# Two blocks of w_up kept on chip between their two uses, and the activation table's root for two tiles of the mixer's norm

## The chip, the cores and the metric

The kernel runs on one core of one Trainium2 chip. The metric is the device time of one execution in microseconds. The profile times every instruction of one execution on the engines: PE is TensorE (matrix products), with PEld its weight loads; DVE is VectorE, ACT is ScalarE, POOL is GpSimd; SP (SyncE) issues the DMAs here, in the order in which they stand in its queue.

## The reference, cut to what matters

Two layers run over 1024 tokens of width 1024. Each has a mixer (three kinds of heads side by side, then an output product) and an MLP; the residual is added after a norm:

```
x = x + g_m * _rmsnorm(y, norm_g[l, 1])          # y: the mixer's output
h = _rmsnorm(x, norm_g[l, 2]) * (1.0 + sc_f) + sh_f
y = jnp.square(jax.nn.relu(h @ w_up[l])) @ w_down[l]
x = x + g_f * _rmsnorm(y, norm_g[l, 3])
```

`w_up[l]` has 1024 rows and 4096 columns. All of it is in f32; the kernel writes each f32 operand as a high and a low part and makes three matrix products of one (`mm3`, L189 to L193).

## The kernel before, in words

**Scheduling.** The Python program says in which order instructions are written and which addresses they use. A scheduler then orders them on each engine by a simulated time; each engine, and SP's DMA queue, runs its own list strictly in order and waits on semaphores.

**Space.** Working tiles come from one arena of 17,856 words per partition (`F_WORDS`). `F.get(a, b)` takes a free run of a·b words, the one released longest ago in program order, and `F.put` releases it. Whoever writes a run again has to wait for the last reader of what lay there before. A load is therefore issued no earlier than the release of its place, and everything behind it in SP's queue waits with it.

**The end of the mixer (`mixer`, L1357).** Tokens are handled in tiles of 128. `out_proj` (L1301) makes the output product of a tile, squares it for the norm (L1321), loads the residual (L1324), forms the inverse root of the mean square (L1327), scales and adds (L1328, L1329) and stores (L1330). Tiles 6 and 7 are the last; their sum and a scratch tile stay on chip (`kept`, four runs of 1024 words). The inverse root is `rsqrt`, L165 to L171: for one column nine small DVE instructions, each needing the one before. The other norms use `rstd` (L182 to L186): a square root on ACT and four small DVE instructions. `renorm` (L1336) loads a tile again (L1346; tiles 6 and 7 are taken from `kept`), norms it (L638 or L636, then L639) and transposes it on PE.

**The up product with fewer multiplications (`mlp_up`, L233).** Tokens are in two halves, the rows of `w_up` in two halves, and its columns in 16 pairs of 128-column groups. For a pair, the four quarter blocks are called a11, a12, a21, a22. The product of a pair is made as two *plain* products (a11 and a12 with the first half of the tokens) and five products of *sums* of blocks with sums of the token blocks. The token sums, called T here, are built by `transp_late` (L200) from tiles 4 to 7: POOL adds (L207, L209), a transpose on PE (L212), DVE differences and splits (L644, L217, L231). The block sums of a pair are made on POOL (L284, L285, L287, L290). Each of the seven operands is split into a high part by ACT (L230) and a low part by DVE (L231) and waits in a ring of four places for its product, twelve matmuls on PE.

**The order in `mlp_up`.** Since T needs the last token tiles, the plain products of the first six pairs (`LEAD`) are made first, interleaved with `renorm` of tiles 4 to 7 (`late`). Then follow the sums of pairs 0 to 5, and from pair 6 on plain and sums together. `todo` lists these 22 steps; `stage` (L265) takes the next one, gets a place and issues its load (L270), one step ahead of `forms` (L273), which yields the split operands. For the first six plain steps only the 128 needed columns are loaded (1024 words, 512 KB); for a sums step, or a whole pair, both groups (2048 words, 1 MB). So pairs 0 to 5 are loaded twice: half, then whole. A plain product leaves `p1` (512 words) in the arena until its sums; results go through two activations (L246, L247) to DRAM (L248).

Of the kernel before, what the change touches and what calls it, by code (L numbers as in the profile page):

```python
# [17 lines left out]
P = 128  # L18
T = 1024
NT = T // P  # L20
D = 1024
KD = D // P
# [3 lines left out]
RMS_EPS = 1e-6  # L26
# [4 lines left out]
WOW = 16  # L31
GROUPS = [2] + [4] * 6 + [2, 4]
LEAD = 6
C_Q, C_K, C_V, C_CQ, C_CKV, C_KR, C_Z, C_XBC, C_DT = 0, 256, 512, 768, 1024, 1152, 1184, 1696, 2464

SLOT = 2048
# [70 lines left out]
class Net:  # L107
# [125 lines left out]
    def mlp_up(self, l, hT, bg, late):  # L233

        nc, F = self.nc, self.F
        w_up = self.i["w_up"][l].rearrange("(k p) f -> p k f", p=P)
        hh, hl = hT
        half = slice(0, 512), slice(512, 1024)  # L240
        B = lambda k, n: tuple(h[:, k * 4:k * 4 + 4, half[n]] for h in hT)
        dma = nc.sync.dma_start

        def store(f, hf, t):

            nc.scalar.activation(t, t, AF.Relu)  # L246
            nc.scalar.activation(t, t, AF.Square)  # L247
            dma(self.d_r[l][f, :, half[hf]], t)  # L248
            F.put(t)


        ring = [tuple(h[:, k, half[1]].rearrange("p (k f) -> p k f", f=P) for h in hT) for k in range(4)]
        turn = [0]

        def cut(src):
            r = ring[turn[0] % 4]
            turn[0] += 1
            self.split(src, *r)
            return r

        N = FF // (2 * P)
        todo = [(i, True, False) for i in range(LEAD)] + [(i, i >= LEAD, True) for i in range(N)]
        staged = []

        def stage():  # L265

            if todo:
                i, plain, sums = todo.pop(0)
                st = F.get(KD, 2 * P if sums else P)
                dma(st, w_up[:, :, i * 2 * P:i * 2 * P + st.shape[2]])  # L270
                staged.append((st, plain, sums))

        def forms():  # L273

            stage()
            st, plain, sums = staged.pop(0)
            a11, a12 = st[:, 0:4, 0:P], st[:, 4:8, 0:P]
            if plain:
                yield cut(a11)
                yield cut(a12)  # L280
            if sums:
                a21, a22 = st[:, 0:4, P:2 * P], st[:, 4:8, P:2 * P]
                s1, s2 = F.get(4, P), F.get(4, P)
                nc.gpsimd.tensor_add(s1, a21, a22)  # L284
                nc.gpsimd.tensor_sub(s2, s1, a11)  # L285
                yield cut(s2)
                nc.gpsimd.tensor_sub(a21, a11, a21)  # L287
                yield cut(a21)
                yield cut(s1)
                nc.gpsimd.tensor_sub(s2, a12, s2)  # L290
                yield cut(s2)
                F.put(s1, s2)
                yield cut(a22)
            F.put(st)

        stage()
        parts = self.chain(*(forms() for _ in range(LEAD + N)))
        queue = [next(parts) for _ in range(3)]

        def product(b):  # L300

            q = next(parts, None)
            if q is not None:
                queue.append(q)
            w, ps = queue.pop(0), self.bank()
            for k in range(4):
                self.mm3(ps, w[0][:, k], w[1][:, k], b[0][:, k], b[1][:, k], k == 0, k == 3)
            return ps

        add = nc.vector.tensor_add  # L310
        T = [tuple(t[:, a] for a in range(2)) for t in self.sums()]
        p1 = {}

        def plain(i):
            ps, p = product(B(0, 0)), F.get(512)
            nc.scalar.copy(p, ps)
            ps, c = product(B(1, 0)), F.get(512)
            add(c, p, ps)
            store(2 * i, 0, c)
            p1[i] = p  # L320

        def sums(i):
            f, p = 2 * i, p1.pop(i)
            ps, u2 = product(T[1]), p
            add(u2, p, ps)
            ps, u3 = product(T[2]), F.get(512)
            add(u3, u2, ps)
            ps = product(T[0])
            add(u2, u2, ps)
            c = F.get(512)  # L330
            add(c, u3, ps)  # L331
            store(f + 1, 1, c)
            ps = product(B(1, 1))
            add(u2, u2, ps)
            store(f, 1, u2)
            ps = product(T[3])
            add(u3, u3, ps)
            store(f + 1, 0, u3)

        for i in range(LEAD):  # L340
            next(late, None)
            next(late, None)
            plain(i)
        self.drain(late)
        for i in range(N):
            if i >= LEAD:
                plain(i)
            sums(i)
            if i > 1:
                next(bg, None)  # L350
                next(bg, None)
# [949 lines left out]
    def out_proj(self, l, t, st, cc, src, dst, g, cT, keep=None):  # L1301

        nc, F = self.nc, self.F
        wo = st["wo"]
        for gg in range(2):
            a = cc[:, 512 + gg * 256:768 + gg * 256]
            nc.gpsimd.tensor_scalar(a, a, st["yrs"][:, 2 * t + gg:2 * t + gg + 1], None, op0=ALU.mult)
        self.transp8(cc, cT[0], cT[1], 0, True)
        if t % 2:
            F.put(st["cc"].pop(t // 2))  # L1310
        yield 1.0
        u = F.get(D)
        ss = self.sm(2, "fss")
        for dh in range(2):
            dd = slice(dh * 512, dh * 512 + 512)
            y = self.bank()
            for k in range(KD):
                self.mm3(y, cT[0][:, k], cT[1][:, k], wo[k][:, 0, dd], wo[k][:, 1, dd], k == 0, k == KD - 1)
                if k % 2:
                    yield 1.3  # L1320
            nc.scalar.activation(u[:, dd], y, AF.Square, accum_out=ss[:, dh:dh + 1])  # L1321
            nc.scalar.copy(u[:, dd], y)
        x = F.get(D)
        nc.sync.dma_start(x, src[t * P:t * P + P])  # L1324
        s = self.sm(1, "fs1")
        nc.vector.tensor_add(s, ss[:, 0:1], ss[:, 1:2])
        rs = self.rsqrt(s, 1, 1.0 / D, RMS_EPS)  # L1327
        nc.vector.scalar_tensor_tensor(u, in0=u, scalar=rs, in1=g, op0=ALU.mult, op1=ALU.mult)  # L1328
        nc.vector.tensor_add(x, x, u)  # L1329
        nc.sync.dma_start(dst[t * P:t * P + P], x)  # L1330
        if keep is None:
            F.put(x, u)
        else:
            keep[t] = x, u
# [262 lines left out]
```

## Time and profile before

| | us |
|---|---|
| time, median of 3 runs | 2828.76 (2823.73 to 2833.22) |
| the profiled execution's own time | 2827.39 |
| its span, first to last instruction | 2825.7 |
| PE busy | 2642.5 |
| DVE busy | 1755.9 |
| ACT busy | 1111.0 |
| POOL busy | 587.5 |

The up product starts at about 743 us in the first layer and at about 2133 us in the second. A row of the timeline reads: start, duration, engine (a q behind it: the queue that issues), line, operation, tiles written and read, shape, number of instructions merged, and in brackets how long the engine had been idle before it and what released it. A row of the windows reads: the stretch, its length, and for each engine its busy time and its instructions, then the granted TensorE clock (1.00 is full), the DMA engines' busy share and the rate. A row of the waits reads: who waited for whom, the microseconds in total, how often, and the longest.

### The profile page before, as it was taken

To read this page: it belongs to the slowest core of one execution; us is meant where nothing else is said; L and a number is where in the kernel's file an instruction comes from. 1 tells how busy PE (TensorE), PEld (TensorE's weight loads), DVE (VectorE), ACT (ScalarE), POOL (GpSimd) and SP (SyncE) were. 2 spreads that over 40 slices of the span, in tenths; PEclk is the share of its full clock that TensorE was granted. 3 is DMA by queue.
4 is the path that set the end of the run, shared out by engine and by line. 5 is a ranking of instruction groups with operands and counts; after the bars stand their busy time and mean duration, and the time that the engine had idled before them with its cause. 6 is when DMAs were issued, how large, how long until landed. Compare 5 with 4: busy or idle time off the path is not lost.

```text
span 2825.7 us, 34756 instructions
## 1 busy us (share of the span) xinstructions
PE 2642.5 (94%) x12530; PEld 2066.1 (73%) x12530; DVE 1755.9 (62%) x3223; ACT 1111.0 (39%) x2145; POOL 587.5 (21%) x517
## 2 busy tenths in 40 slices
PE   5799999899879999999999999988997999999998
PEld 4677776676757777777778777765766888888886
DVE  7767666544867777756585576664459654643435
ACT  5243443544534446121143433354445455621212
POOL 1441233310333220000021113342003522000002
PEclk9899988899989999999999998888998999999999
DMA  6441212322345546534331121132133432541313
GB/s 225 116 137 51 94 50 61 110 73 84 101 150 165 158 148 216 179 122 151 107 119 48 56 91 63 54 101 86 52 105 104 153 116 101 177 149 65 120 47 102
DMA packets 268527, 311.54 MB, mean 110 GB/s; under 512 B 28674, under 2 KB 212164, under 8 KB 268356
## 3 DMA queue, kind: packets, MB, share of 16 engines
q1 hardware_dynamic: 268356, 309.32, 34.0%
q8 instruction: 99, 1.62, 0.2%
q14 instruction: 72, 0.59, 0.1%
HBM read 242.85 MB, written 66.43 MB: 109 GB/s over the span
## 4 chain that ended last, share of the span: by engine, by line
PE 65%; DVE 11%; DMA 7%; issue 2%; ACT 2%; POOL 1%; SPq 0%; DVEq 0%; ACTq 0%; POOLq 0%
PE bank_b L191 9%; PE bank_b L193 9%; PE bank_b L192 9%; PE bank_s L191 8%; PE bank_s L192 8%; PE bank_s L193 8%; PE bank_s L962 3%; DVE split L231 2%; PE bank_a L909 2%; PE bank_t L922 2%; DVE arena_f L570 2%; DMA arena_f<-in_w_ada 1%; DMA d_r<-arena_f 1%; PE bank_s L656 1%; PE bank_a L938 1%
## 5 line engine op out<-in xcount | busy, mean ns | idle before, releaser
L191 PE MATMUL bank_b<-split 128*128 128x512 f32 (+2 forms) x1824 | 728.5, 400 | 51.0 <-ACT split L230 33.1
L192 PE MATMUL bank_b<-split 128*128 128x512 f32 (+2 forms) x1824 | 709.6, 389 | 3.5 <-DVE split L231 3.1
L193 PE MATMUL bank_b<-split 128*128 128x512 f32 (+2 forms) x1824 | 706.5, 389 | 2.9 <-DVE split L231 2.9
L230 ACT CAST split<-arena_f 128x512 fp32r<-128x512 f32 (+1 forms) x424 | 305.8, 747 | 678.3 <-PE bank_s L192 425.8
L191 PE MATMUL bank_s<-split 128*128 128x512 f32 (+2 forms) x1152 | 456.1, 398 | 18.3 <-DVE arena_f L390 6.7
L192 PE MATMUL bank_s<-split 128*128 128x512 f32 (+2 forms) x1152 | 451.2, 392 | 4.4 <-DVE split L231 1.8
L191 PEld LDWEIGHTS bank_b<-split 128*128 128x128 f32 x1824 | 354.1, 194 | 129.5 <-ACT split L230 34.8
L193 PE MATMUL bank_s<-split 128*128 128x512 f32 (+2 forms) x1152 | 448.2, 389 | 0.0
L231 DVE TENSOR_TENSOR split<-arena_f,split 128x512 fp32r<-128x512 f32 (+1 forms) x424 | 381.7, 919 | 92.8 <-ACT split L230 92.0
L193 PEld LDWEIGHTS bank_b<-split 128*128 128x128 f32 x1824 | 352.7, 193 | 71.6 <-DVE split L231 5.0
L192 PEld LDWEIGHTS bank_b<-split 128*128 128x128 f32 x1824 | 354.7, 194 | 68.5 <-issue 4.9
L408 DVE TENSOR_TENSOR arena_f<-arena_f,bank_s 128x1024 f32<-128x1024 f32 x126 | 153.5, 1218 | 230.9 <-PE bank_s L193 230.9
L191 PEld LDWEIGHTS bank_s<-split 128*128 128x128 f32 (+1 forms) x1152 | 218.4, 190 | 73.8 <-DVE arena_f L390 7.4
L192 PEld LDWEIGHTS bank_s<-split 128*128 128x128 f32 (+1 forms) x1152 | 219.5, 191 | 50.4 <-DVE split L231 3.5
L193 PEld LDWEIGHTS bank_s<-split 128*128 128x128 f32 (+1 forms) x1152 | 219.1, 190 | 43.4 <-issue 0.2
L897 ACT ACTIVATE arena_f<-bank_s,nm 128x128 f32<-128x128 f32 (+3 forms) x192 | 141.8, 740 | 191.8 <-DVE nm L896 160.8
L896 DVE TENSOR_REDUCE nm<-bank_s 128x1 f32<-128x128 f32 (+3 forms) x192 | 142.2, 752 | 118.8 <-PE bank_s L1111 64.5
L570 DVE SCALAR_TENSOR_TENSOR arena_f<-arena_f,cond 128x128 f32<-128x128 f32 x448 | 161.7, 387 | 71.4 <-DMA arena_f<-in_b_ada 32.9
L246 ACT ACTIVATE arena_f<-arena_f 128x512 f32<-128x512 f32 x128 | 80.8, 632 | 141.6 <-DVE arena_f L331 69.6
L962 PE MATMUL bank_s<-split 32*128 32x512 f32 (+3 forms) x576 | 124.0, 390 | 12.3 <-ACT arena_f L897 9.1
L925 ACT COPY arena_f<-bank_t 128x512 f32<-128x512 f32 (+1 forms) x160 | 86.8, 542 | 114.1 <-PE bank_t L922 100.9
L696 POOL TENSOR_TENSOR arena_f<-arena_f 128x1024 f32<-128x1024 f32 x14 | 33.6, 2399 | 454.0 <-ACT rstd_y L182 340.0
(281 smaller groups left out, 3207.0 us busy)
## 6 DMA issues: line engine op xcount, KB each, us to landing
arena_f<-in_w_ada SPq DMA_DIRECT2D x80, 512.0 KB
d_r<-arena_f SPq DMA_DIRECT2D x128, 256.0 KB
arena_f<-in_w_up SPq DMA_DIRECT2D x32, 1024.0 KB
arena_f<-in_w_down SPq DMA_DIRECT2D x64, 512.0 KB
arena_f<-d_r SPq DMA_DIRECT2D x64, 512.0 KB
arena_f<-d_x SPq DMA_DIRECT2D x36, 512.0 KB
d_x<-arena_f SPq DMA_DIRECT2D x23, 512.0 KB
arena_f<-in_w_in SPq DMA_DIRECT2D x20, 512.0 KB
```

Source lines behind the costliest of these rows:

```text
L191: mm(out, wh, xh, start=start, stop=False)
L192: mm(out, wh, xl, start=False, stop=False)
L193: mm(out, wl, xh, start=False, stop=stop)
L230: self.nc.scalar.copy(hi, src)
L231: (eng or self.nc.vector).tensor_sub(lo, src, f32(hi))
L246: nc.scalar.activation(t, t, AF.Relu)
L408: nc.vector.tensor_add(y[t], y[t], ps)
L570: nc.vector.scalar_tensor_tensor(acc, in0=w[:, k], scalar=self.cond[:, k:k + 1], in1=acc, op0=ALU.mult, op1=ALU.add)
L896: nc.vector.tensor_reduce(nm, S[:, 0:n], axis=AX.X, op=ALU.max, negate=True)
L897: nc.scalar.activation(p[:, 0:n], S[:, 0:n], AF.Exp, bias=nm, accum_out=ls)
L925: nc.scalar.copy(held, ps[:, 0:w])
L962: nc.tensor.matmul(S[mp][:, c0:c1], Q[rw, a, tok], K[rw, b, c0:c1], start=a == b, stop=a == 1 and c1 < n)
```

## The change

The first two plain steps (`KEEP = 2`) load the whole pair, 2048 words and 1 MB instead of 1024 words and 512 KB. They don't release it; it is held in `whole` until the sums of that pair, which take it from there and issue no load. And `out_proj` of tiles 6 and 7 (those with `keep`) calls `rstd` instead of `rsqrt`.

```diff
+KEEP = 2
...
         todo = [(i, True, False) for i in range(LEAD)] + [(i, i >= LEAD, True) for i in range(N)]
-        staged = []
+        staged, whole = [], {}
...
                 i, plain, sums = todo.pop(0)
-                st = F.get(KD, 2 * P if sums else P)
-                dma(st, w_up[:, :, i * 2 * P:i * 2 * P + st.shape[2]])
-                staged.append((st, plain, sums))
+                keep = i < KEEP and not sums
+                if i in whole:
+                    st = whole.pop(i)
+                else:
+                    st = F.get(KD, 2 * P if sums or keep else P)
+                    dma(st, w_up[:, :, i * 2 * P:i * 2 * P + st.shape[2]])
+                if keep:
+                    whole[i] = st
+                staged.append((st, plain, sums, keep))
...
-            st, plain, sums = staged.pop(0)
+            st, plain, sums, keep = staged.pop(0)
...
-            F.put(st)
+            if not keep:
+                F.put(st)
...
-        rs = self.rsqrt(s, 1, 1.0 / D, RMS_EPS)
+        rs = self.rsqrt(s, 1, 1.0 / D, RMS_EPS) if keep is None else self.rstd(s)
```

## The prediction

> **What bounds the kernel now.** I read the page first, then who waited for whom on PE around the start of each up product, then the timeline of each engine there, and last the windows for the clock.
>
> ```profile
> span 2825.7 us, 34756 instructions
> PE 2642.5 (94%) x12530; PEld 2066.1 (73%) x12530; DVE 1755.9 (62%) x3223; ACT 1111.0 (39%) x2145; POOL 587.5 (21%) x517
> ...
> PE bank_b L191 <- ACT split L230: 20.9, 2, 19.0
> ```
>
> PE is busy 94% of the span, so a change that adds or takes little PE work can only act where PE stands idle or runs slowly. The third row is PE's longest wait between 700 and 850 us: 19.0 us at one matmul, for a split weight. Its place is the step from the plain products to the sums:
>
> ```profile
> 784.78 1.04 PE L212 MATMUL bank_s<-ident,arena_f 128*128 128x128 f32 x8
> 804.84 0.79 PE L191 MATMUL bank_b<-split 128*128 128x512 f32 x1 [19.02 <-ACT split L230]
> ...
> 2176.92 1.04 PE L212 MATMUL bank_s<-ident,arena_f 128*128 128x128 f32 x8
> 2185.60 0.79 PE L191 MATMUL bank_b<-split 128*128 128x512 f32 x1 [7.65 <-ACT split L230]
> 2189.45 0.79 PE L192 MATMUL bank_b<-split 128*128 128x512 f32 x1 [3.06 <-DVE split L231]
> ```
>
> In both layers PE ends the plain products with the transposes of token tile 7 (L212), at 785.8 and 2178.0, and then waits for the first sums. Behind the split stands POOL, which makes the block sums, and behind POOL the load:
>
> ```profile
> 774.16 1.37 POOL L209 TENSOR_TENSOR arena_f<-arena_f 128x512 f32<-128x512 f32 x1
> 791.70 1.44 POOL L284 TENSOR_TENSOR arena_f<-arena_f 128x512 f32<-128x512 f32 x1 [16.17 <-DMA arena_f<-in_w_up]
> ...
> 801.53 1.26 POOL L284 TENSOR_TENSOR arena_f<-arena_f 128x512 f32<-128x512 f32 x1
> ...
> 2180.63 1.52 POOL L284 TENSOR_TENSOR arena_f<-arena_f 128x512 f32<-128x512 f32 x1 [15.92 <-DMA arena_f<-in_w_up]
> ...
> 729.39 0.34 SPq L1346 DMA_DIRECT2D arena_f<-d_x  x1
> ...
> 743.50 0.38 SPq L270 DMA_DIRECT2D arena_f<-in_w_up  x1
> ...
> 770.14 0.38 SPq L270 DMA_DIRECT2D arena_f<-in_w_up  x1
> ...
> 785.85 0.38 SPq L270 DMA_DIRECT2D arena_f<-in_w_up  x1
> ...
> 792.27 19.81 SPq L270 DMA_DIRECT2D arena_f<-in_w_up  x4
> ...
> 2162.15 0.38 SPq L270 DMA_DIRECT2D arena_f<-in_w_up  x1
> ...
> 2173.24 1.12 SPq L270 DMA_DIRECT2D arena_f<-in_w_up  x2
> ...
> 2191.14 8.93 SPq L270 DMA_DIRECT2D arena_f<-in_w_up  x2
> ```
>
> The row at 770.14 is the half load of pair 5, the last plain one; those from 785.85 on are whole. The first whole load goes out at 785.85, when PE is already done, and POOL gets it at 791.70: 5.85 us for 1 MB. PE's first sums product starts 3.3 us behind the L284 at 801.53, the third, so by the times the pair that PE needs came third. In the second layer the pair comes first, issued at 2173.24. Either way the load, not the work, is late.
>
> The idle time also costs clock:
>
> ```profile
> 804.80:809.40 4.60, 4.21 (x9) 2.91 (x10) 4.00 (x3) 1.24 (x2) 2.29 (x2) 0.50 0.00 0
> ...
> 2185.60:2195.20 9.60, 6.54 (x15) 4.78 (x16) 9.06 (x8) 1.76 (x3) 6.51 (x4) 0.50 0.29 93
> 860.00:980.00 120.00, 115.27 (x502) 89.87 (x501) 93.88 (x194) 54.22 (x97) 37.08 (x39) 1.00 0.51 162
> ```
>
> At full clock a matmul takes 115.27/502 = 0.23 us. In the first stretch, at clock 0.50, PE got 9 done by 809.4, worth 2.1 us; so the sums stand as if they had started at full clock at 807.3. In the second layer: 15 by 2195.2, worth 3.45 us, as if started at 2191.75.
>
> **Part 1: the loads that go.** With the change, pairs 0 and 1 lie in the arena when the sums begin; per layer two 1 MB loads leave SP's queue, and two 512 KB loads become 1 MB. The wait for the load goes entirely. What is late next is T, the token sums, of which tile 7 is the last part; it comes from DVE, and DVE is full:
>
> ```profile
> 743.40:780.80 37.40, 33.88 (x147) 27.10 (x146) 36.64 (x60) 22.38 (x41) 13.52 (x6) 0.91 0.23 78
> ...
> 2135.30:2173.20 37.90, 32.53 (x142) 26.02 (x141) 37.79 (x68) 22.97 (x41) 10.16 (x6) 0.93 0.20 69
> ...
> 785.04 0.69 DVE L318 TENSOR_TENSOR arena_f<-arena_f,bank_b 128x512 f32<-128x512 f32 x1 [4.26 <-PE bank_b L193]
> 785.86 0.69 DVE L644 TENSOR_TENSOR arena_f<-bank_s,arena_f 128x512 f32<-128x512 f32 x1
> ...
> 790.74 2.96 DVE L231 TENSOR_TENSOR split<-arena_f,split 128x512 fp32r<-128x512 f32 x3
> ```
>
> DVE works 36.64 of 37.40 us up to the norm of tile 7, and 37.79 of 37.90 in the second layer. So however the steps are reordered, T is ready no earlier than this work plus what is left: the add at 785.04 (0.7 us), tile 7's instructions from 785.86 to the first of the three last splits at about 791.7 (5.9 us, T for the first product), and two weight splits of about 0.7 us (1.4). That is 8.0 us, less 1.1 us from part 2: 6.9 us. First layer: 780.8 + 6.9 = 787.7, against 807.3: **-19.6 us**. Second layer: 2173.2 + 6.9 = 2180.1, against 2191.75: **-11.65 us**. PE, done at 785.8 and 2178.0, then waits about 2 us.
>
> **Part 2: the root.** For tiles 6 and 7 nine small DVE instructions become four and a root on ACT:
>
> ```profile
> 742.83 0.14 DVE L165 TENSOR_SCALAR rs_m<-fs 128x1 f32<-128x1 f32 x1
> ...
> 746.71 0.27 DVE L170 TENSOR_SCALAR rs_t<-rs_y,rs_m 128x1 f32<-128x1 f32 x1
> ...
> 765.84 1.27 DVE L1328 SCALAR_TENSOR_TENSOR arena_f<-arena_f,rs_y 128x1024 f32<-128x1024 f32 x1
> ...
> 776.01 0.14 DVE L183 TENSOR_SCALAR rstd_m<-nss 128x1 f32<-128x1 f32 x1
> ...
> 779.50 1.28 DVE L639 SCALAR_TENSOR_TENSOR arena_f<-arena_f,rstd_y 128x1024 f32<-128x1024 f32 x1
> ```
>
> The five instructions saved are 0.14 to 0.27 us each: 0.7 to 1.35 us a tile, I take 1.1. Much more is their queueing: between larger work, the nine take from 742.83 to 765.84, 23 us; the same tile's `rstd` takes 3.5 us (776.01 to 779.50). So tile 7's chain can end up to 19 us earlier. This frees no DVE time, which is why part 1 goes by DVE's total; but it lets the transposes of tile 7 stand ahead of the last plain products on PE. Without it T would come as now, 791.7. The root adds one small instruction to ACT, which works 22.38 of 37.40 us there: nothing. I count no table load for it, since `renorm` takes roots in the same stretch.
>
> **Part 3: what the held pairs cost.** In front: the up loads are ahead of the load of a token tile in SP's queue (729.39), for which ACT waited:
>
> ```profile
> 734.27 1.06 ACT L638 ACTIVATE split<-arena_f 128x1024 fp32r<-128x1024 f32 x1 [3.05 <-DMA arena_f<-d_x]
> ...
> 741.45 1.97 PE L212 MATMUL bank_s<-ident,arena_f 128*128 128x128 f32 x8 [3.15 <-DVE arena_f L639]
> ```
>
> PE's wait of 3.15 us stands behind that norm. A further 512 KB ahead of it takes 0 (hidden) to 5.85/2 = 2.9 us; I take 1.5 a layer: **+3 us**. The larger cover is that the first product starts at 743 and the first load goes out at 711.
>
> In the middle: POOL's sums for pairs 0 and 1, now at 791 to 806 beside idle engines, will run when POOL is free, from 775.5, beside full DVE. That this costs DVE time:
>
> ```profile
> 2180.95 5.10 DVE L217 TENSOR_TENSOR arena_f<-arena_f 128x512 f32<-128x512 f32 x3
> 2185.98 8.82 DVE L231 TENSOR_TENSOR split<-arena_f,split 128x512 fp32r<-128x512 f32 x7
> ```
>
> These ten, beside POOL's block sums, took 13.9 us; ten at the 0.69 us of the L644 row would take 6.9. The bounds are 0 and the difference, 7.0 us a layer. I take 2.5, nearer to 0, since part of POOL's sums can fall behind T: **+5 us**. The Trainium skill speaks against the change here: "SBUF — State Buffer", section "Who interferes with whom", says that a DVE instruction with two SBUF inputs contends with a GpSimd instruction that reads SBUF, by an exclusive lock held for the whole instruction. By that rule the sums' full duration would be DVE's loss; the trace agrees in kind (1.39 us each against 0.69).
>
> Space: the two held pairs take 4096 of 17,856 words, and 3072 more than before lie there during the plain products. By counting gets and puts about 1,950 words stay free at the tightest point, so later half loads may get places that are released later. If they do not, nothing; if they do, the rivals below.
>
> **The sum.** -19.6 - 11.65 + 3 + 5 = -23.2 us. The profiled execution took 2827.39 us, 1.4 us less than the median of 2828.76. 2827.39 - 23.2 = 2804.2; against the median 2805.6. I predict **2806**; its own range, with the bounds of the front and POOL terms (not all at their ends at once), is 2796 to 2816.
>
> **The rivals.**
> *DVE does not bind.* If the order lets T be ready when PE ends, and pair 5's half load stops being late, the sums start with the plain end less the idle that its late load (770.14) makes today:
>
> ```profile
> 774.89 0.50 PE L191 MATMUL bank_b<-split 128*128 128x512 f32 x1 [1.84 <-ACT split L230]
> 778.32 0.79 PE L193 MATMUL bank_b<-split 128*128 128x512 f32 x1 [1.69 <-DVE split L231]
> ...
> 2167.50 0.50 PE L191 MATMUL bank_b<-split 128*128 128x512 f32 x1 [4.56 <-ACT split L230]
> ```
>
> That is 785.8 - 3.5 = 782.3 and 2178.0 - 4.6 = 2173.4: -25.0 - 18.4 + 3 = -40, 2788. Against it stand the full DVE rows.
> *POOL takes DVE's time in full*: 7.0 instead of 2.5 us a layer, -14.2 us, 2815. For it: POOL has nothing else to do from 775.5.
> *Pair 5's half load falls one place back* in the line of loads, to 785.85 and 2173.24, since its space is held. From issue to the end of the plain products it was 785.8 - 770.14 = 15.7 us and 15.8 us. They would then end at 801.5 and 2189.0: -5.8 - 2.7 + 3 = -5.5, 2823: no change that can be told.
> *Slower: it falls two or three places back*, to the later loads of the same line (792.27 and the one behind it; 2191.14). The plain products end at about 808.4 and 2206.9: +1.1 + 15.2 + 3 = +19, 2848. This decides from an issue later than 791.6 in the first layer (807.3 less 15.7) and 2175.9 in the second. For it: loads wait for places today already. Against: by program order the places of tile 6 and of two earlier half loads are released before it.
>
> **How the numbers follow.** Chances: forecast 0.52, DVE not binding 0.11, POOL in full 0.13, one place back 0.12, two or more 0.12. The measurement can tell about 0.3%, 8.5 us. Faster: 0.52 + 0.11 + 0.09 of the POOL case = 0.72. Same: the other 0.04 and one place back, 0.16. Slower: 0.12. The range runs from 2790, inside the best case, to 2825, behind one place back; it leaves out the slower case and half of the best one.
>
> **What would show it.** Right: no wait of PE above 5 us at the first sums product; four loads of w_up fewer; POOL's first L284 ahead of PE's last plain product; clock 1.00 where it was 0.50; tile 7's L1328 some 10 to 19 us nearer to its square. Wrong: an idle PE in front of the plain products of pairs 2 to 5 with a load of w_up behind it (space), or PE waiting for L217 or L231 by more than 8 us (DVE), or an L212 of tile 4 later than 743 (front).

## The result: slower by half a per cent, and the profile after

| | before | after |
|---|---|---|
| median of 12 runs each, us | 2826.45 (2818.20 to 2836.52) | 2841.55 (2829.22 to 2856.83) |
| ratio, 95% interval | | 1.0054 (1.0029 to 1.0080) |
| the profiled execution: its time, its span | 2827.39, 2825.7 | 2842.88, 2841.2 |

The change costs about 15 us; forecast was a gain of 23. The head of the page of after:

```profile
span 2841.2 us, 34709 instructions
...
PE 2653.4 (93%) x12530; PEld 2072.1 (73%) x12530; DVE 1759.5 (62%) x3203; ACT 1113.1 (39%) x2149; POOL 581.2 (20%) x517
```

PE has the same 12530 instructions and DVE and ACT the intended 20 fewer and 4 more; PE's busy time grew by 11 us. Of this some 7 is clock: PE was busy at half clock for 226 us, in before for 211, and half of the 15 more is time lost. Lines of after are one higher than those of before up to about L264 and seven or eight higher behind. PE's longest waits between 700 and 850 us:

```profile
PE bank_b L192 <- ACT split L231: 15.6, 3, 14.0
PE bank_b L194 <- DVE split L232: 2.3, 1, 2.3
```

Still one long wait for a split weight, 14.0 us in place of 19.0. But it stands elsewhere. PE's timeline of after, both layers (in brackets the idle time and its releaser):

```profile
775.30 0.79 PE L192 MATMUL bank_b<-split 128*128 128x512 f32 x1 [13.97 <-ACT split L231]
...
778.78 0.79 PE L194 MATMUL bank_b<-split 128*128 128x512 f32 x1 [2.26 <-DVE split L232]
...
2170.52 4.92 PE L213 MATMUL bank_s<-ident,arena_f 128*128 128x128 f32 x24 [6.07 <-DVE rstd_y L187]
...
2189.32 0.79 PE L192 MATMUL bank_b<-split 128*128 128x512 f32 x1 [13.87 <-ACT split L231]
...
2206.67 0.50 PE L193 MATMUL bank_b<-split 128*128 128x512 f32 x1 [3.31 <-DVE split L232]
```

The wait at the first sums is gone: in the first layer the last plain add runs at 794.4 and the first add of the sums at 795.6. The new 14 us stand ahead of the *plain* product of pair 4, in both layers. What PE waited for there, on ACT (first layer):

```profile
761.29 2.70 ACT L231 CAST split<-arena_f 128x512 fp32r<-128x512 f32 x5 [7.12 <-DMA arena_f<-in_w_up]
...
774.64 1.65 ACT L231 CAST split<-arena_f 128x512 fp32r<-128x512 f32 x3
```

The split at 774.64 waits for the semaphore of the load that SP issued at 770.11, 512 KB for pair 4 (SP's list has the six loads in the order 3, 2, 0 whole, 1 whole, 5, 4). SP's timeline and, behind it, its longest wait for such a load:

```profile
757.30 13.20 SPq L275 DMA_DIRECT2D arena_f<-in_w_up  x2
```
```profile
SPq L275 <- DVE split L232: 19.5, 3, 12.4
```

SP held that load back for 12.4 us until DVE's low part L232 of a token tile had left its place. By the arena's addresses pair 4's half load got 1024 words of which half had just been one of tile 5's working tiles (the others a finished plain result, already stored); in before it got the token rows of tile 4, which come free a tile earlier, and it was pair 5's half load that got working tiles of tile 5. While PE idled, its clock fell; windows of after:

```profile
764.80:781.90 17.10, 4.34 (x9) 2.98 (x10) 17.07 (x19) 6.83 (x12) 9.00 (x6) 0.50 0.15 47
...
2178.00:2195.00 17.00, 5.68 (x13) 4.33 (x14) 15.90 (x21) 8.57 (x16) 6.92 (x5) 0.50 0.29 83
```

Clock 0.50 for 17 us in each layer, where before had 0.50 around the first sums. DVE worked 17.07 of 17.10 us: the places that SP waited for came free at DVE's pace.

**Stretches.** To compare kernels I cut each profiled execution at five marks: first plain copy of the up product, start of the down product, first norm of the second layer's output product, first plain copy of the second layer, start of its down product. PE's idle time is the length of a stretch less PE's busy time in the windows.

| us | up, layer 0 | down 0 and mixer 1 | output product 1 | up, layer 1 |
|---|---|---|---|---|
| before | 352.4 | 863.3 | 175.2 | 320.7 |
| after | 348.3 | 876.5 | 185.4 | 328.5 |

Only the first column gained, by 4.1 us. The other three lost 13.2, 10.2 and 7.8, and the first two of these lie ahead of the second layer's up product.

### The profile page after: what moved, and what is told of

Same layout as the page of the kernel before. It is cut to its first block, busy times and chain, and to the rows that moved or that the text cites. A ratio compares the mean times of both kernels' runs of the same rounds, so it can differ in the third digit from the quotient of the medians.

```text
span 2841.2 us, 34709 instructions
## 1 busy us (share of the span) xinstructions
PE 2653.4 (93%) x12530; PEld 2072.1 (73%) x12530; DVE 1759.5 (62%) x3203; ACT 1113.1 (39%) x2149; POOL 581.2 (20%) x517
## 5 line engine op out<-in xcount | busy, mean ns | idle before, releaser
L232 DVE TENSOR_TENSOR split<-arena_f,split 128x512 fp32r<-128x512 f32 (+1 forms) x424 | 385.1, 929 | 94.1 <-ACT split L231 88.3
L905 ACT ACTIVATE arena_f<-bank_s,nm 128x384 f32<-128x384 f32 (+4 forms) x192 | 142.1, 742 | 187.1 <-DVE nm L904 152.7
L578 DVE SCALAR_TENSOR_TENSOR arena_f<-arena_f,cond 128x128 f32<-128x128 f32 x448 | 155.4, 378 | 76.9 <-DMA arena_f<-in_w_ada 46.9
L970 PE MATMUL bank_s<-split 32*128 32x512 f32 (+3 forms) x576 | 122.9, 386 | 10.5 <-ACT arena_f L905 7.2
```

What stands on the lines that cost most here:

```text
L232: (eng or self.nc.vector).tensor_sub(lo, src, f32(hi))
L578: nc.vector.scalar_tensor_tensor(acc, in0=w[:, k], scalar=self.cond[:, k:k + 1], in1=acc, op0=ALU.mult, op1=ALU.add)
L905: nc.scalar.activation(p[:, 0:n], S[:, 0:n], AF.Exp, bias=nm, accum_out=ls)
L970: nc.tensor.matmul(S[mp][:, c0:c1], Q[rw, a, tok], K[rw, b, c0:c1], start=a == b, stop=a == 1 and c1 < n)
```

## The experiments

Two theories at the start. *Space*: the held pairs push later loads onto late places. *Root*: the new root delays something at the end of the mixer. All ratios below are to runs of before that alternate with them on the same chip (medians 2821.98 to 2823.23, 23 to 29 runs each), for 6 to 12 runs of each kernel; that of after is the one above. The kernels ran in groups, each on another chip, so between groups the ratios compare better than the times.

**One part alone.** `keep_only` holds the pairs and keeps the old root:

```diff
-        rs = self.rsqrt(s, 1, 1.0 / D, RMS_EPS) if keep is None else self.rstd(s)
+        rs = self.rsqrt(s, 1, 1.0 / D, RMS_EPS)
```

> The change with its loads alone: pairs 0 and 1 held, the old root (nine DVE instructions) in out_proj. Space theory (the held places push the load of token tile 5 and the half load of pair 4 behind the token sums of tile 4 and 5): slower than before by 8 to 25 us, with PE waits over 8 us in front of a plain product in at least one layer. Root theory (the new root reorders the engines and delays the last tiles; the loads alone help): faster by 10 to 25 us, no PE wait over 5 us between the first plain product and the first sums.

`root_only` has the root and holds nothing; the diff of the pairs is undone.

> The change with its root alone: no pair held, all loads as before. Space theory: -6 to +2 us, the wait at the first sums still there (15 to 20 us in the first layer, 5 to 10 in the second). Root theory: slower by 10 to 25 us.

Measured: pairs alone 2812.76, ratio 0.9955 (0.9930 to 0.9979); root alone 2826.72, 1.0006 (0.9986 to 1.0026). So neither part alone is slower. With the pairs held, adding the root costs 28.8 us. That is no sum of two separate costs, and both theories missed. Space is not enough: the pairs alone show the same wait of 14.46 and 13.82 us ahead of pair 4 and still gain. Nor is the root: alone it should have cost 10 to 25 us, and no change can be told.

**Space without data.** `space_only` (old root) holds the places of pairs 0 and 1 but loads only halves into them, releases them at the sums and loads the pairs whole into places free by then:

```diff
-                    st = whole.pop(i)
+                    F.put(whole.pop(i))
+                    st = F.get(KD, 2 * P)
+                    dma(st, w_up[:, :, i * 2 * P:i * 2 * P + 2 * P])
...
-                    dma(st, w_up[:, :, i * 2 * P:i * 2 * P + st.shape[2]])
+                    c = 2 * P if sums else P
+                    dma(st[:, :, 0:c], w_up[:, :, i * 2 * P:i * 2 * P + c])
```

> The places of the change without its saved loads: pairs 0 and 1 get 2048 words each at their plain step and hold them until their sums, but only the half is loaded there, and the whole is loaded again for the sums into a new place, as before; old root. Space theory: slower than before by 15 to 40 us, the same late loads as in the change (token tile 5 and the half load of pair 4 issued 10 us or more later than before against the first plain product) and a wait at the first sums besides. Root theory, or a theory by which the size of the first loads is at fault: within 5 us of before.

2802.47, ratio 0.9920 (0.9893 to 0.9946): 20 us faster, a clear miss of both theories on the time. In the first layer PE does wait 16.64 us ahead of pair 4's plain product, for a split of a half load issued only at 767.35, as the space theory expected; in the second no such wait is left. The wait for the first whole load goes here too, since the load finds a place that has been free for long and goes out before the plain products end. So keeping the *data* isn't what removes that wait. A long stretch far from the change is short as well: down 0 and mixer 1 took 841.7 us.

**One pair.** `last_one` (new root) holds only pair 5 and makes its sums first:

```diff
-KEEP = 2
+KEEP = 1
...
-        todo = [(i, True, False) for i in range(LEAD)] + [(i, i >= LEAD, True) for i in range(N)]
+        order = [*range(LEAD - KEEP, LEAD), *range(LEAD - KEEP), *range(LEAD, N)]
+        todo = [(i, True, False) for i in range(LEAD)] + [(i, i >= LEAD, True) for i in order]
...
```

> Only the last plain pair (5) is loaded whole and held, and its sums come first, before those of pairs 0 to 4; new root. Nothing is held while tiles 4 to 7 are worked on up to the place of pair 5's own load. Space theory: faster than before by 8 to 25 us, since the wait at the first sums goes and no token load is late; pair 5's load takes about 2 us longer. Root theory: slower by 5 to 20 us, as the change.

2807.86, 0.9961 (0.9939 to 0.9982): 15 us faster, as the space theory forecast here. Less space held, no wait above 7.2 us in either up product; again mixer 1 is short, 847.4 us.

**A first try at the far stretch.** The working tiles of the second layer's mixer get other addresses when the first layer's up product ends in another state of the arena. The addresses of after and `keep_only` are the same there (876.5 and 877.1 us), as are those of before and `root_only` (863.3 and 863.3), which looked like a cost of 13 us for places. `same_places` is after with a list of 793 addresses of before, `keep_places` the same in `keep_only`:

```diff
...
-        at = self._find(m, top)
+        k, self.count = self.count - 677, self.count + 1
+        at = PLACES[k] if 0 <= k < len(PLACES) else None
+        if at is None or any(self.used[at:at + m]):
+            at = self._find(m, top)
```

> After, with one thing undone: from the sixth block load of layer 0's sums to the end of layer 1's mixer the arena hands out the addresses of before (a fixed list), so the mixer of layer 1 has before's places again; held pairs and root stay. Theory of places: the stretch from layer 0's down product to layer 1's first output norm takes 863 us plus or minus 3 as in before (863.4) and with the root alone (863.3), not 876.4 as in after and 877.1 with the pairs alone; the time is about 13 us under after, near 2828 (1.000 to 1.002 of before). Rival, chance of the clock: the 13 us are where the half clock fell in two profiled executions; the stretch lies anywhere from 860 to 880 and the median stays with after, 2838 to 2842 (1.004 to 1.006).

> The same list of addresses in the kernel that holds the pairs but keeps the old root. Theory of places: the stretch falls from 877.1 to 863 plus or minus 3 and the time from 2812.8 to about 2800 (0.990 to 0.993 of before). Rival, chance of the clock: the time stays at 2810 to 2815 (0.995 to 0.997).

`forgotten` is before with one line more behind the first layer's down product:

```diff
+            F.stamp = [0] * F.n
```

> Before, without any part of the change; only the arena forgets after layer 0's down product when each run of words was released, so that the mixer of layer 1 gets other places. Same work, same loads. Theory of places: that stretch's 841.7, 847.4, 863 and 877 us in four placements say that placement alone moves it by some 10 us either way; the ratio to before leaves 1.000 by over 0.003 and the whole difference lies in layer 1's mixer. Rival: places do not matter where nothing is held; 1.000 plus or minus 0.003.

Measured: `same_places` 2838.54, 1.0042 (1.0023 to 1.0060), the stretch 872.0; `keep_places` 2827.18, 1.0026 (1.0003 to 1.0049), the stretch 862.2; `forgotten` 2819.14, 0.9994 (0.9977 to 1.0012), the stretch 867.8. The theory falls in this form: the times did not follow. Two reasons are visible. The list began inside the first layer's up product and made that longer, 360.8 and 351.3 us against 348.3 and 341.1 in the kernels it was put into. And the 13 us were mostly clock: by the granted clock, after ran 113 us of the stretch at half clock, before 85, `same_places` with before's addresses 106; half of such time is lost. PE idled *less* in after, as these two windows show:

```profile
1099.50:1962.80 863.30, 824.61 (x3965) 642.03 (x3965) 543.37 (x1071) 295.91 (x603) 150.38 (x138) 0.95 0.33 104
```
```profile
1082.70:1959.20 876.50, 844.99 (x3977) 656.50 (x3977) 555.60 (x1084) 296.62 (x605) 148.84 (x141) 0.94 0.32 103
```

Before, then after: 863.30 less 824.61 is 38.7 us idle, 876.50 less 844.99 is 31.5.

**More space.** `returned` releases the scratch of tiles 6 and 7 and the gain row before the up product:

```diff
-            keep[t] = x, u
+            F.put(u)
+            keep[t] = x
...
-            x, u = src[t]
+            x, u = src[t], F.get(D)
...
+        F.put(g)
...
-        F.put(g, *nxt)
+        F.put(*nxt)
```

> After, but the scratch tiles of tiles 6 and 7 and the gain row (3072 words) are released before the up product instead of at its late part, so the loads of pairs 4 and 5 get places that come free one tile earlier. Theory of space: the wait of 14 us ahead of pair 4's plain product (13.97 us in layer 0, 13.87 in layer 1) falls to 7 us or less in both layers, and from the first plain copy to the down product layer 0 takes 341 or less (348.3 in after), layer 1 322 or less (328.5). Rival, VectorE is the bound there: its token work ends no sooner, the wait stays at 12 to 14 us and moves by less than 2. The total is not forecast closely, since the mixer of layer 1 gets other places too: 2815 to 2840.

2844.36, 1.0072 (1.0044 to 1.0100). The wait on a late load is gone in both layers; others took its place, the longest 7.46 us for a DVE add in the first layer, 6.65 and 6.35 in the second. The up products took 350.7 and 321.4: the second as forecast, the first not; the time is above the forecast 2815 to 2840.

**What the root delays.** Now I laid the two kernels with the same addresses, after and `keep_only`, side by side, at the end of the second layer's mixer. ACT of after:

```profile
2104.83 1.04 ACT L646 ACTIVATE split<-arena_f 128x1024 fp32r<-128x1024 f32 x1
2105.78 0.19 ACT L646 ACTIVATION_READ_ACCUMULATOR split<-arena_f 128x1 f32 x1
2112.74 0.60 ACT L1329 ACTIVATE arena_f<-bank_b 128x512 f32<-128x512 f32 x1 [6.78 <-PE bank_b L194]
...
2119.86 0.30 ACT L183 ACTIVATE rstd_y<-fs,eps 128x1 f32<-128x1 f32 x1
...
2120.95 0.48 ACT L183 ACTIVATE rstd_y<-nss,eps 128x1 f32<-128x1 f32 x2
```

ACT of `keep_only`, the same place:

```profile
2093.80 0.19 ACT L646 ACTIVATION_READ_ACCUMULATOR split<-arena_f 128x1 f32 x1
2093.89 0.47 ACT L183 ACTIVATE rstd_y<-nss,eps 128x1 f32<-128x1 f32 x2
2099.50 0.60 ACT L1329 ACTIVATE arena_f<-bank_b 128x512 f32<-128x512 f32 x1 [5.14 <-PE bank_b L194]
```

L646 are the squares of token tiles 2 and 3, the two L183 on `nss` their roots. In `keep_only` they follow at once. In after the root of tile 6 (`fs`) stands ahead of them in ACT's list, and it needs tile 6's output product. ACT idles 6.78 us with two roots at hand, and they run 15 us after their squares. DVE's norms of these two tiles and SP's queue follow; DVE of after, then SP of after:

```profile
2105.62 1.28 DVE L647 SCALAR_TENSOR_TENSOR arena_f<-arena_f,rstd_y 128x1024 f32<-128x1024 f32 x1
2115.89 1.29 DVE L652 TENSOR_TENSOR arena_f<-bank_s,arena_f 128x512 f32<-128x512 f32 x2 [8.98 <-PE bank_s L664]
...
2125.27 2.48 DVE L647 SCALAR_TENSOR_TENSOR arena_f<-arena_f,rstd_y 128x1024 f32<-128x1024 f32 x2
```
```profile
2124.72 0.34 SPq L1338 DMA_DIRECT2D d_x<-arena_f  x1
2131.94 0.37 SPq L275 DMA_DIRECT2D arena_f<-in_w_up  x1
2134.42 0.34 SPq L1354 DMA_DIRECT2D arena_f<-d_x  x1
2146.38 0.34 SPq L1338 DMA_DIRECT2D d_x<-arena_f  x1
...
2160.82 0.32 SPq L1354 DMA_DIRECT2D arena_f<-d_x  x1
```

The norms at 2125.27 let PE transpose tiles 2 and 3, which frees the place of the whole load at 2131.94; behind that stands the load of token tile 4 (2134.42), behind its work that of tile 5 (2160.82), and PE's wait of 6.07 us for tile 5's root at 2170.52. `keep_only` is 12.0 us earlier at the end of the last square, but 24.0 and 24.1 us earlier at the two token loads (2110.43 and 2136.71): 12 us are lost on the way.

Why is tile 6's root ahead? `rstd` takes its three one-column tiles by name from sets of four. In the order in which the program is written, tile 6's root comes between those of tiles 1 and 2; if the scheduler gives out the tiles of one set in that order, the roots of tiles 2 and 3 can't be put ahead of tile 6's. The old root drew from sets of its own and could be passed. This was inferred from the order of the instructions; the next run tests it. `own_tiles` is after with one thing changed:

```diff
-    def rstd(self, ssq, y=None):
+    def rstd(self, ssq, y=None, own=False):
...
+        if own:
+            m, t = (self.small.tile([P, 16], F32, tag=f"rs_{c}", name=f"rs_{c}", bufs=3)[:, 0:1] for c in "mt")
+            y = self.sm(1, "rs_y")
...
-        rs = self.rsqrt(s, 1, 1.0 / D, RMS_EPS) if keep is None else self.rstd(s)
+        rs = self.rsqrt(s, 1, 1.0 / D, RMS_EPS) if keep is None else self.rstd(s, own=True)
```

> After, pairs held and root kept, but the root of tiles 6 and 7 takes its three one-column tiles from the sets that the old root used, not from the set that the roots of tiles 0 to 5 share. Theory of the shared set: in after ScalarE's root of tile 6 (2119.86 us, it waits for the output product) stands in its list ahead of the roots of tiles 2 and 3, whose squares were done at 2105.97; their norms run at 2125.27, and the load of token tile 5 goes out at 2160.82. With sets of their own those two roots pass: the norms run within 3 us of the squares, the load of token tile 5 goes out about 12 us earlier against the products, and the time falls to that of the pairs alone or a little under, 2804 to 2816 (0.992 to 0.997 of before). Rival, the pairs and the root both ask for space or for ScalarE: the time stays at 2830 to 2842 (1.002 to 1.006).

2805.83 (2799.82 to 2816.24), ratio 0.9941 (0.9921 to 0.9961), inside the forecast: 35.7 us under after, or 32 by the two ratios. ACT of `own_tiles` (L650 and L187 are the square and the root):

```profile
2084.10 1.04 ACT L650 ACTIVATE split<-arena_f 128x1024 fp32r<-128x1024 f32 x1
2085.05 0.19 ACT L650 ACTIVATION_READ_ACCUMULATOR split<-arena_f 128x1 f32 x1
2085.14 0.47 ACT L187 ACTIVATE rstd_y<-nss,eps 128x1 f32<-128x1 f32 x2
2090.77 0.60 ACT L1333 ACTIVATE arena_f<-bank_b 128x512 f32<-128x512 f32 x1 [5.16 <-PE bank_b L198]
...
2097.86 0.30 ACT L187 ACTIVATE rs_y<-fs,eps 128x1 f32<-128x1 f32 x1
```

The two roots run directly behind their squares and tile 6's comes last. SP of `own_tiles` sends token tile 4 at 2101.73, ahead of the store of tile 6, and tile 5 at 2127.64:

```profile
2101.73 0.34 SPq L1358 DMA_DIRECT2D arena_f<-d_x  x1
2106.04 14.26 SPq L1342 DMA_DIRECT2D d_x<-arena_f  x2
...
2127.64 0.32 SPq L1358 DMA_DIRECT2D arena_f<-d_x  x1
```

From the last square (2105.78 and 2085.05) to tile 5's load it is 42.6 us, against 55.0 in after: the 12 us are back. In the first layer it is 36.3 against 46.9. The Trainium skill states the condition, in "PSUM — Partial Sum Buffer", section "Engine vs sequencer instructions": the queues of ScalarE, VectorE and GpSimd are strictly first in, first out. The rows agree: ACT idled 6.78 us with ready work behind a waiting instruction.

The same edit in three other kernels: the root without pairs (`root_own`), `last_one` (`last_own`), and `space_only`, which thereby gets the new root (`space_own`).

> The root alone, no pair held, with tiles of its own as well. Theory of the shared set: the 8 us that the root alone costs at full clock (2696 against 2688) go; 2812 to 2822 (0.996 to 1.000 of before) where the root with shared tiles gave 2826.7. Rival: the short root is worth nothing either way; 2823 to 2830.

> The kernel that holds only pair 5 and sums it first (2807.9 with the shared set), with tiles of its own for the root. Theory of the shared set: some 5 to 10 us less, 2796 to 2804 (0.990 to 0.994 of before). Rival: no change, 2804 to 2812.

> The kernel that only holds the places of pairs 0 and 1 and loads them twice (2802.5 with the old root), with the root in tiles of its own. Theory of the shared set: the root in its own tiles costs nothing; 2795 to 2805 (0.990 to 0.994 of before). Rival, the root itself brings the loss of the change: 2815 or more.

Measured: `root_own` 2806.65, 0.9946 (0.9922 to 0.9970), 20 us under `root_only` and more than forecast; `last_own` 2805.24, 0.9939 (0.9919 to 0.9958), only 2.6 us under `last_one`, a miss; `space_own` 2787.61, 0.9883 (0.9850 to 0.9916), 15 us under `space_only` and better than forecast, though the two ratios' intervals overlap. `own_tiles` and `root_own` show the cost of the shared set, and `root_own` that the root in its own tiles is a gain over before's; `last_own` shows no cost. `root_own` holds nothing and is as fast as `own_tiles`: once the root has its own tiles, the held pairs bring no difference that can be told. So the two parts don't add up: with nothing held the root's gain, 15 us, and the shared set's cost, 20 us, nearly cancel, while with the pairs held the cost is far larger than the gain.

The traces show where the cost comes from in some of these. In the second layer of `root_only` the two roots are held up too, from the last square at 2094.53 to 2109.32, and token tile 5's load goes out at 2123.41; in `root_own` that load goes out at 2099.5. In `last_one` they are held up as long, from 2082.88 to 2097.03, but that load had gone out at 2083.41, ahead of them.

**What is left of space.** In `own_tiles` PE still waits ahead of pair 4:

```profile
769.72 0.80 PE L196 MATMUL bank_b<-split 128*128 128x512 f32 x1 [12.34 <-ACT split L235]
...
2155.22 0.80 PE L196 MATMUL bank_b<-split 128*128 128x512 f32 x1 [12.77 <-ACT split L235]
```

`returned_own` joins `returned` and `own_tiles`. `own_far` is `own_tiles` with a list of 691 addresses of `space_own`, from the last third of the first layer's up product to the end of the second layer's mixer, so behind the place where the first lists did harm; `before_far` is before with the same list.

> Pairs held, root in its own tiles, and the 3072 words of tiles 6 and 7's scratch and the gain row released before the up product, so that the loads of pairs 4 and 5 get places that come free one tile earlier. Theory of space: the wait on a split behind a block load ahead of pair 4's plain product, 12.3 us in layer 0 and 12.8 in layer 1 with the places of after, is gone or under 5 us in both layers; PE's idle time from the first plain copy to the down product falls from 20 and 17 us to 15 or less. The time 2795 to 2806 (0.990 to 0.994), the mixer of layer 1 adding its own some microseconds either way. Rival, VectorE's token work is the bound there: other waits of the same sum take its place, PE's idle time stays at 17 us or more in both layers, and the time at 2800 to 2815.

> Pairs held, root in its own tiles; from the last third of layer 0's up product to the end of layer 1's mixer the arena hands out the addresses of the kernel that only held the places. Theory that places cost idle time in that mixer: TensorE idles 23 to 25 us from layer 0's down product to layer 1's first output norm, as in the two kernels with those places (24.5 and 23.0), not 34.3 as with its own; with the half clock that goes with it the time falls by 10 to 20 us to 2786 to 2796 (0.987 to 0.991). Rival, chance: idle 31 to 37 us and 2802 to 2810.

> Before, nothing held and the old root; only the addresses from the last third of layer 0's up product to the end of layer 1's mixer are those of the same list. Theory that places cost: TensorE idles 23 to 25 us in that stretch, not 38.7, and the time falls by 10 to 20 us to 2802 to 2812 (0.993 to 0.997) with not one instruction of the change. Rival, chance: idle 36 to 39 us and a ratio of 1.000 plus or minus 0.002.

`returned_own`: 2832.26, 1.0039 (1.0013 to 1.0065), slower than `own_tiles` by 26 us. The rival is right on the waits, and the time is above both forecasts: 142.6 us on average are lost to the half clock, 120.1 in `own_tiles`. No wait on a load is left ahead of pair 4, but PE idles 20.7 and 18.6 us in the up products, of which 12.1 and 15.2 are in front of a copy; PE, then ACT of `returned_own`:

```profile
773.00 0.80 PE L196 MATMUL bank_b<-split 128*128 128x512 f32 x1 [9.49 <-ACT arena_f L328]
```
```profile
767.44 0.62 ACT L235 CAST split<-arena_f 128x512 fp32r<-128x512 f32 x1 [3.93 <-DVE arena_f L222]
770.56 1.82 ACT L235 CAST split<-arena_f 128x512 fp32r<-128x512 f32 x3 [2.50 <-DVE arena_f L222]
772.36 0.58 ACT L328 COPY arena_f<-bank_b 128x512 f32<-128x512 f32 x1
```

The copy that PE waits for (L328, it empties a bank) stands in ACT's list behind splits of the token sums, which wait for DVE's differences (L222). With the load on time PE idles as long as in `own_tiles` (20.1 and 17.3 us), now for DVE's token work. Why more clock is lost is not shown.

With `returned_own` four pairs of kernels differ in the root's tiles alone. Own tiles are faster in all four: by 35.7 us with pairs held, 20.1 with the root alone, 12.1 in `returned`, 2.6 in `last_one`, which is 32, 17, 9 and 6 us by the ratios. Only the first two are clear of the noise, so the size of the cost hangs on the kernel around it.

`own_far`: 2777.16 (2775.96 to 2792.73), 0.9847 (0.9813 to 0.9881), better than forecast; `before_far`: 2808.66, 0.9944 (0.9920 to 0.9969), faster by 14 us without one instruction of the change, its time as forecast. The stretch of down 0 and mixer 1 in `own_tiles`, `own_far` and `before_far`:

```profile
1072.80:1939.40 866.60, 832.33 (x3977) 646.81 (x3977) 552.13 (x1084) 295.71 (x605) 147.43 (x141) 0.95 0.33 104
```
```profile
1071.00:1911.00 840.00, 817.59 (x3953) 637.96 (x3952) 536.22 (x1068) 292.32 (x600) 148.66 (x139) 0.96 0.33 104
```
```profile
1090.50:1940.90 850.40, 824.53 (x3977) 642.96 (x3977) 541.74 (x1077) 296.19 (x605) 148.22 (x139) 0.95 0.33 104
```

PE idles 34.3, 22.4 and 25.9 us, against 38.7 in before. So places do cost idle time there, and it follows the list of addresses: with before's 35.7 to 39.0 in five kernels, with those of after 31.5 to 34.3 in three, with those of `space_own` 22.4 to 25.9 in four. In `own_far` the up product of the second layer shrank too, 311.0 against 319.3 us; the wait of 12.77 us ahead of pair 4 is gone there, the longest left being 4.92 us for a DVE add one product earlier, with the same program and only the places other. It is the fastest kernel of this study, 45 us under before.

| | holds | root's tiles | addresses far on | median us | ratio to before |
|---|---|---|---|---|---|
| after | pairs 0, 1 | shared | own | 2841.55 | 1.0054 (1.0029 to 1.0080) |
| `keep_only` | pairs 0, 1 | old root | as after | 2812.76 | 0.9955 (0.9930 to 0.9979) |
| `own_tiles` | pairs 0, 1 | own | as after | 2805.83 | 0.9941 (0.9921 to 0.9961) |
| `root_own` | nothing | own | as before | 2806.65 | 0.9946 (0.9922 to 0.9970) |
| `before_far` | nothing | old root | of `space_own` | 2808.66 | 0.9944 (0.9920 to 0.9969) |
| `space_own` | places only | own | of `space_own` | 2787.61 | 0.9883 (0.9850 to 0.9916) |
| `own_far` | pairs 0, 1 | own | of `space_own` | 2777.16 | 0.9847 (0.9813 to 0.9881) |

## Why the prediction was wrong, by its own steps

**Part 1, the loads that go.** That the load wait at the first sums vanishes was right (SP issues 40 loads of `w_up` instead of 44), and so was "DVE is full" as the next bound: 17.07 of 17.10 us in the new gap. The size was not. From the first plain copy to the first add of the sums, before took 63.3 and 60.2 us, after 61.2 and 66.6: 2.1 gained in the first layer, 6.4 lost in the second, where 19.6 and 11.65 were forecast as gains. With the root's tiles apart it is 52.7 and 58.1, so 10.6 and 2.1 gained. The forecast took DVE's work as one sum that could be done in any order. It can't: the place of a load comes free at one certain instruction of it.

**Part 2, the root: the step that failed.** "The root adds one small instruction to ACT ...: nothing." The instruction does take 0.30 us. But it waits for tile 6's output product, and through the shared set of tiles it is ahead of two ready roots. This is the 32 to 36 us between after and `own_tiles`, and the sign of the result. Of the difference, the stretches of the two profiled executions show 12.1 in the first up product, 5.7 at the output product and 9.2 in the second up product; the mixer's 9.9 is clock, 113 against 89 us at half clock with the same addresses. No loading of ACT's function tables comes in: there are 8 such loads in before and 8 in after. The prediction asked what queues behind a *moved DMA*, and did not ask it of the added ACT instruction. That tile 7's chain ends earlier was right: its scaling (L1328 in before) starts 3.3 us behind the start of its last square in after, 25.4 us in before (first layer). In after this gained nothing on balance; how much of `root_own`'s 15 us it is was not measured apart.

**Part 3, the cost of holding.** "Space: ... if they do not, nothing; if they do, the rivals below." They did: pair 4's half load fell onto a place of tile 5's token work, 13.97 and 13.87 us, and so the sign showed that the prediction had named for space, an idle PE in front of a plain product with a load behind it. The rivals with a half load some places back describe what happened to the pairs, though for pair 4, not 5, and alone it is not slow: `keep_only` is 10 us faster than before. That the slower one's 2848 lies near the measured 2841.55 is therefore luck. These rivals had 0.24 in all and should have been the main case, since 1,950 free words against half loads of 1024 leave hardly a choice of place. The front term (1.5 us a layer) hardly shows in `own_tiles`: PE's waits ahead of the transposes L217 are 1.84 and 1.79 us in the second layer and under 1.5 in the first, where before had 3.15 in the first layer and 1.24 in the second. For POOL's sums 5 us of DVE's time were forecast; none shows in `keep_only`, where the same 3223 DVE instructions are busy for 1755.4 us, against 1755.9 in before.

**The number.** `own_tiles`, the change as it was meant, comes out at 2805.8 where 2806 was forecast, but by luck and not by that sum: its first up product gained 16.2 us, the second 1.4, and `root_own` shows the same time with no pair held.

**Left open.** Why one list of addresses leaves PE 12 to 13 us less idle in the second mixer was not followed to single waits. `last_own` against `last_one` shows no cost of the shared set; in the second layer the early load of tile 5 can explain it, in the first it was not followed up. Why the shared set costs more with the pairs held is open too.

## What to carry to other kernels

A small instruction on an idle engine is not free if it waits: look at what is ready behind it in that engine's list, and at which of its tiles come from a set that others draw from in program order. Holding a tile to save a load costs the places of the loads in between, so count free places at the time of each of them, not bytes. And where addresses come from a least-recently-released rule, any change of allocation moves waits in code far away; compare by stretches, and try one list of addresses in both kernels before a far difference is put down to the change.

## What the runs showed of the hardware

Most of the scatter between runs of one kernel is PE's clock. Each run lists its span and mean clock. In the 12 runs of after, span times clock is 2696.8 us on average and scatters by 3.5, the rest, lost to the half clock, is 143.5 and scatters by 10.5; the correlation of span and clock is -0.95. In before (104 runs) the two are 2688.6 and 133.4, in `own_tiles` 2685.4 and 120.1. So of the 35 us between after and `own_tiles`, 11 are work and waits and 23 are clock. The first 550 us run the same instructions in all kernels here, and in 17 profiled executions they hold 82 to 116 us at half clock. A difference of 10 us in one stretch of one profile is therefore no finding; PE's idle time in the second mixer was one, and repeated within 4 us for one list of addresses.

The Trainium skill describes the clock in "TensorE: Matmul & The Clock Gate", Part 1: two states, half and full, set from activity in windows of about 3.4 us that run freely, so that the cost varies from run to run. The stretches at 0.50 agree, 17.1 and 17.0 us being five such windows. Its remark that the ramp is under 1% of a typical span is about warming up; over the whole of this kernel the clock's loss in after is 143.5 of 2840 us, 5%.
